# A gate's modulation moved ahead of the FFN, weight buffers that start their turn anew, and a second set of banks

## The chip, the cores and the metric

The kernel runs on one core of one Trainium2 chip. The time is that of the device, in microseconds (us), for one execution on that core. The engines are named as the profile names them: PE (TensorE, matmuls), DVE (VectorE), ACT (ScalarE), POOL (GpSimd) and SP (SyncE, which here only issues transfers). PEld is the loading of PE's weights.

## The reference

One block of an encoder: 512 tokens, width 2048. A vector `c` gives six modulation vectors. The block mixes tokens by two kinds of attention (global with grouped keys, and over a neighbourhood in a grid), merges both with sigmoid gates, projects the result with `w_out`, and adds a gated feed-forward net (FFN) of width 5632.

```python
c_act = jax.nn.silu(c)
mod = c_act @ w_ada[l] + b_ada[l]
sh1, sc1, g1, sh2, sc2, g2 = [m[:, None, :] for m in jnp.split(mod, 6, axis=-1)]
h = rms_norm(x, norm1_w[l]) * (1.0 + sc1) + sh1
...
merged = jax.nn.sigmoid(ga) * (ya @ w_oa[l]) + jax.nn.sigmoid(gb) * (yb @ w_ob[l])
x = x + g1 * (merged @ w_out[l])
h2 = rms_norm(x, norm2_w[l]) * (1.0 + sc2) + sh2
ff = (jax.nn.silu(h2 @ w_ffn_gate[l]) * (h2 @ w_ffn_up[l])) @ w_ffn_down[l]
x = x + g2 * ff
return rms_norm(x, final_w)
```

`g2`, the second gate, is 2048 numbers: `c_act` (2048) times a 2048 x 2048 part of `w_ada`, which is 16 MB. It is needed only at the very end, when the FFN's result is added.

## The kernel before

**Arithmetic.** Each fp32 product is made of three matmuls on split numbers (`mm3`, L140 to L143): hi times hi, hi times lo, lo times hi. A weight unit of 512 KB is loaded into a buffer `raw` by a DMA on SP's queue (L148); ACT copies it to the high half of a buffer `whl` (L133), DVE subtracts that for the low half (L134), and 24 matmuls of 128x512 use it.

**Buffers and their turn.** `buffer` (L106 to L111) counts the tiles taken of a tag. There are four `raw` and three `whl` buffers in the pool `wp`. From w_out on, a second pool `wq` (L730) adds one `raw` and two `whl`, so that the turn runs over five of each; the counter goes on from where it stands, and the last numbers of a turn are those in `wq`. The memory of `wq` was that of `p_y`: the attention outputs `y0` to `y15` and the scratch tiles `o` of the heads' projections.

**Order of the work.** The program is one list of instructions, which a scheduler turns into one queue for each engine; every engine works its queue in order. Work that isn't part of the main flow is put in generators (`bg`), and `pump` (L166) advances them by `pace["steps"]` at each weight unit or call; `soon` holds closing steps, to be run a given number of pumps later.

**Stages by time (from the profiled execution).** Input projections and the first modulation to about 260 us; global attention to 560; neighbourhood attention and gates to about 905. Then the heads' output projections (L715 to L727): 16 calls, each of 48 matmuls (two weight units), whose results DVE multiplies with the gates (L710), adds (L721) and splits into `m0` to `m7` (L726 and L727 for the last). Then w_out (L805 to L814): four passes over column blocks of 512, `cc` 0 to 3, where the units of a pass take one of `m0` to `m7` each. After it come the norm and the FFN's hidden layer in an arrangement that saves matmuls (seven products instead of eight, whose input sums `ta` and `tb` are formed from weights on DVE), from about 1310 to 2150. The first down pass (L1118 to L1125) is four column passes of four units each, each filling four banks of PSUM that ACT copies out (L1120). The groups of the down projection follow, to 2480, and the last part with the norm to the end.

**The second gate.** `ada_gate` (L320) makes one quarter (512 columns) of a gate: an accumulator `acc` is cleared by POOL, its first row set to the bias by a DMA, eight loads of 512 KB each (L274) bring two blocks of 128 rows, and DVE adds each, times `c_act`, into `acc` (L298). At the end one matmul with ones sums over the partitions (`total`). The first gate runs so beside the attention, loaded on SP's queue. The second ran during the FFN: loads on POOL's queue, one load ahead of its use, one accumulator, totals in bank T, and one advance at each step of a group's inner loop but the first two.

Of the kernel before, what the change touches and what calls it, by code (L numbers as in the profile page):

```python
# [13 lines left out]
F32 = mybir.dt.float32  # L14
F32R = mybir.dt.float32r
AF = mybir.ActivationFunctionType
# [3 lines left out]
P = 128  # L20
D = 2048
T = 512
NT = T // P
KT = D // P
# [63 lines left out]
def encoder_block(ctx: ExitStack, tc, xp, xT, c, w_ada, ada1_w, b_ada, norm1_w, w_in, q_norm_w, k_norm_w, tb,  # L88
                  w_oa, w_ob, w_out, norm2_w, w_gate, w_up, w_down, final_w, rope, wmask, out):
    nc = tc.nc  # L90
    V, S, G = nc.vector, nc.scalar, nc.gpsimd
# [30 lines left out]
    def bank(tag):  # L122
        return ps.tile([P, 512], F32, tag=tag, name=tag, bufs={"mm": 4, "S": 2, "T": 1, "Y": 1}[tag])
# [34 lines left out]
    bg = []  # L158
# [4 lines left out]

    pace = {"steps": 1}

    def pump():  # L166
        due = [f for n, f in soon if n <= 0]
        soon[:] = [(n - 1, f) for n, f in soon if n > 0]
        for f in due:
            f()  # L170
        if later:
            later.pop(0)()
        for _ in range(pace["steps"]):
            advance()
# [84 lines left out]
    t2 = const.tile([P, KT], F32, name="t2")  # L259

    accp = aside
    ada_room = {"bank": "Y", "bufs": 2, "ahead": 0, "queue": nc.sync}

    def ada_units(cols, w):

        nj = len(cols)
        nk = 1024 // (nj * w)

        def load(k0):
            raw = raw_tile()  # L270
            r4 = raw.rearrange("p (k c n) -> p k c n", k=nk, c=nj)
            for j, col in enumerate(cols):
                src = w_ada[k0 * P:(k0 + nk) * P, col:col + w]
                ada_room["queue"].dma_start(r4[:, :, j], src.rearrange("(k p) n -> p k n", p=P))  # L274
            return [(k0 + e, raw[:, e * nj * w:(e + 1) * nj * w]) for e in range(nk)]

        ready = []
        for k0 in range(0, KT, nk):
            ready.append(load(k0))
            yield ready.pop(0) if len(ready) > ada_room["ahead"] else None  # L280
        yield from ready

    def ada_acc(cols, w, bias):


        acc = accp.tile([P, 512], F32, tag="acc", name="acc", bufs=ada_room["bufs"])[:, :len(cols) * w]
        if bias:
            G.memset(acc, 0.0)
            nc.sync.dma_start(acc[0:1, :], b_ada[:, cols[0]:cols[0] + w])
        for parts in ada_units(cols, w):  # L290
            if parts is None:
                yield None
                continue
            for k, part in parts:
                if k == 0 and not bias:
                    V.tensor_scalar(acc, part, cact[:, k:k + 1], None, op0=ALU.mult)
                else:
                    V.scalar_tensor_tensor(acc, part, cact[:, k:k + 1], acc, op0=ALU.mult, op1=ALU.add)  # L298
            yield None
        yield acc  # L300
# [21 lines left out]
    def ada_gate(col, q, dst):  # L322

        for acc in ada_acc((col + q * 512,), 512, True):
            if acc is None:
                yield

        def total():
            y = bank(ada_room["bank"])
            nc.tensor.matmul(y, ones, acc, start=True, stop=True)  # L330
            o = io.tile([P, 512], F32, tag="io", name="ada_o")
            V.tensor_copy(o[0:1, :], y[0:1, :])
            nc.sync.dma_start(dst[q], o[0:1, :])

        soon.append((ada_room["bufs"] - 1, total))
        if ada_room["bufs"] == 1:
            yield

    def rows(dst, src):
        for q in range(4):  # L340
# [260 lines left out]
    bg.extend(ada_mod(3 * D, 4 * D, k, 2, (s2, b_sc2, n2, t2, b_sh2)) for k in range(0, KT, 2))  # L601
    g1_d, g2_d = ([dram.tile([1, 512], F32, name=f"g{n}d{q}") for q in range(4)] for n in (1, 2))
    bg.extend(ada_gate(2 * D, q, g1_d) for q in range(4))
    pace["steps"] = 2
    gates(sg_b, GB, 0, 8)
    pace["steps"] = 1
# [105 lines left out]
        return evac  # L712

    turn = itertools.cycle(("mm", "mm", "S"))
    for j in range(0, KT, 2):  # L715
        ma, mb = [], []
        for w, ys, sg, to in ((w_oa, yT[:8], sg_a, ma), (w_ob, yT[8:], sg_b, mb)):
            tag = next(turn)
            form1([w], j * P, 2, ys, [[bank(tag), bank(tag)]], gated(sg[j:], to))
        for e in range(2):  # L720
            V.tensor_add(ma[e], ma[e], mb[e])  # L721
            (mh, ml), o3 = (t.t for t in mT[j + e]), ma[e].rearrange("p (t n) -> p t n", t=2)
            if j + 2 < KT:
                split(mh, ml, o3)
            else:
                V.tensor_copy(mh, o3)  # L726
                V.tensor_sub(ml, o3, mh)  # L727
    p_y.release()
    aside.release()
    wq = tc.alloc_tile_pool(name="wq", bufs=1, side="right", reuse_waits="tile")  # L730

    x2_d = dram.tile([P, NT, D], F32, name="x2d")
# [83 lines left out]
        pump()  # L816
    norm((2, 3))
    gpool.release()
    accp = tc.alloc_tile_pool(name="accp", bufs=1, side="left", reuse_waits="tile")
    ada_room.update(bank="T", bufs=1, ahead=1, queue=nc.gpsimd)  # L820

# [62 lines left out]
    def group7(wsrc, xs, order, dst):  # L886

        bk = {r: bank(BANK[r]) for r in ORDER}
        for n, s in enumerate(order):
            w = wsrc(s)  # L890
            if n > 1:
                pump()
            for r in ORDER:
                (wh, wl), (xh, xl) = w[r], xs[s][r]
                for q in range(2):
                    for c in range(2):
                        o = bk[r][:, c * 256:(c + 1) * 256]
                        cs = slice(c * P, (c + 1) * P)
                        first, last = n == 0 and q == 0 and c == 0, n == len(order) - 1 and q == 1
                        mm3(o, wh[:, q, cs], wl[:, q, cs], xh[:, q], xl[:, q], first, last, skip_group_check=True)  # L900
        p = {r: b.rearrange("p (c n) -> p c n", c=2) for r, b in bk.items()}
        (d11, d12), (d21, d22) = dst
        with tc.high_priority():
            p1 = io.tile([P, 512], F32, tag="io", name="p1").rearrange("p (c n) -> p c n", c=2)
            S.activation(p1, p[1], AF.Copy)
            V.tensor_add(d11, p[2], p1)
            V.tensor_add(d21, p[6], p1)
            V.tensor_add(d12, p[5], d21)
            V.tensor_add(d12, p[3], d12)  # L909
            V.tensor_add(d21, p[7], d21)  # L910
            V.tensor_add(d22, p[5], d21)
            V.tensor_sub(d21, d21, p[4])
# [60 lines left out]
        e1, _ = c_tile(F32R, "e1")  # L973
        early[1] = ff_pair(0, 1, [e1[:, :1024], e1[:, 1024:]], nc.sync)

    bg.extend(ada_gate(5 * D, q, g2_d) for q in range(4))
    for n in range(FU):
        cs = []
        for w in (w_gate, w_up):
# [19 lines left out]
            V.tensor_mul(cs[1][:, sl], cs[1][:, sl], cs[0][:, sl])  # L999
        (nc.sync if n < FU - 1 else nc.gpsimd).dma_start(ff_d[n], cs[1])  # L1000

    while bg or soon:
        pump()
    wbufs["at"] = 0
    for p in (c_p, f_x[1], f_x[0], ca, f_x[3], f_x[2], accp, p_m):
        p.release()
    p_s = form_pool("p_s", "left")
    p_e = form_pool("p_e", "right")
# [108 lines left out]
    xs = FF(0, early, 48)  # L1117
    for cc in range(4):  # L1118
        o = acc_tile()
        form2(w_down, cc * 512, xs, lambda i, b: S.activation(o[:, i], b, AF.Copy), r0=0)  # L1120
        nc.gpsimd.dma_start(acc_d[cc], o)
        if cc == 0:
            xs.pairs.pop(0)
            xs.pairs.pop(1)
            bg.extend(sforms(j, 2 + j) for j in range(3))  # L1125
# [134 lines left out]
```

## Time and profile before

| what | value |
|---|---|
| time, median of 3 runs | 2630.73 us (2626.41 to 2637.36) |
| time of the profiled execution | 2638.57 us |
| its span in the profile | 2636.8 us |
| mean granted clock of PE | 0.993 |
| DVE, ACT, POOL busy | 73%, 39%, 5% of the span |
| transfers | 458.78 MB, mean 174 GB/s |

The profile's page gives busy times by engine, the chain of work that ended last, and groups of instructions. Windows give the same busy times for stretches of time, with the clock that PE was granted there (1.00 is full speed). Waits name what an engine stood still for. In the timeline a bracket shows how long the engine was idle before a row and what ended it.

### The profile page before, as it was taken

How to read it: one execution, taken by the hardware profiler on the slowest of the kernel's cores; microseconds unless marked ns; L12 is line 12 of the kernel's file. 1: busy time of each engine (PE TensorE's matmuls, PEld its weight loads, DVE VectorE, ACT ScalarE, POOL GpSimd, SP SyncE). 2: the span in 40 equal slices, each digit the busy share in tenths (PEclk: the TensorE clock that was granted, in tenths of full speed). 3: DMA queues.
4: the chain of work that ended last, by engine and by line, in shares of the span. 5: the costliest groups of instructions: out<-in, count | busy, mean ns of one | idle time of the engine just before them, and what ended most of it. 6: DMA issues, size and time to landing. Idle time of an engine off the chain costs nothing.

```text
span 2636.8 us, 40994 instructions
## 1 busy us (share of the span) xinstructions
PE 2575.5 (98%) x16569; PEld 2328.0 (88%) x16569; DVE 1912.8 (73%) x2710; ACT 1030.0 (39%) x1404; POOL 119.0 (5%) x166
## 2 busy tenths in 40 slices
PE   6999999999999999999999999999999999999998
PEld 5788888888788888788999999999999988999997
DVE  7985786666746544336798888888888875678767
ACT  5223544223333332226744444444444453434233
POOL 0100000001010000011000000000000000000000
PEclk9999999999999999999999999999999999999999
DMA  8864245974735844546454444444444456447473
GB/s 323 305 236 144 65 156 175 294 232 148 229 104 169 262 156 144 180 131 218 123 161 144 129 144 152 131 142 136 137 146 150 145 167 216 160 156 236 153 255 104
DMA packets 247855, 458.78 MB, mean 174 GB/s; under 512 B 16113, under 2 KB 102497, under 8 KB 239217
## 3 DMA queue, kind: packets, MB, share of 16 engines
q1 hardware_dynamic: 229504, 364.86, 43.1%
q0 software_dynamic: 16672, 88.09, 9.8%
q10 hardware_dynamic: 1488, 3.20, 0.3%
q8 instruction: 130, 2.13, 0.3%
q14 instruction: 61, 0.49, 0.1%
HBM read 412.03 MB, written 44.06 MB: 173 GB/s over the span
## 4 chain that ended last, share of the span: by engine, by line
PE 86%; DVE 6%; DMA 5%; issue 1%; ACT 1%; SPq 0%; DVEq 0%; ACTq 0%; POOLq 0%
PE mm L141 18%; PE mm L142 18%; PE mm L143 18%; PE S L141 6%; PE S L143 6%; PE S L142 6%; PE Y L141 3%; PE Y L142 3%; PE Y L143 3%; DVE whl L134 2%; DMA raw<-in_w_in 2%; DMA raw<-in_w_up 1%; DVE acc L298 1%; PE T L143 1%; PE T L142 1%
## 5 line engine op out<-in xcount | busy, mean ns | idle before, releaser
L133 ACT ACTIVATE whl<-raw 128x1024 fp32r<-128x1024 f32 (+1 forms) x483 | 464.5, 963 | 893.3 <-PE mm L143 302.9
L134 DVE TENSOR_TENSOR whl<-raw,whl 128x1024 fp32r<-128x1024 f32 (+1 forms) x483 | 532.7, 1114 | 312.1 <-ACT whl L133 302.2
L298 DVE SCALAR_TENSOR_TENSOR acc<-raw,cact,acc 128x512 f32<-128x512 f32 x248 | 187.2, 755 | 27.8 <-DMA raw<-in_w_ada 22.4
L133 ACT ACTIVATE whl<-tb 128x1024 fp32r<-128x1024 f32 x104 | 110.6, 1063 | 177.8 <-PE S L143 136.0
L133 ACT ACTIVATE whl<-ta 128x1024 fp32r<-128x1024 f32 x104 | 110.5, 1062 | 163.6 <-PE mm L143 123.0
L134 DVE TENSOR_TENSOR whl<-ta,whl 128x1024 fp32r<-128x1024 f32 x104 | 127.4, 1225 | 39.8 <-ACT whl L133 39.8
L134 DVE TENSOR_TENSOR whl<-tb,whl 128x1024 fp32r<-128x1024 f32 x104 | 127.0, 1221 | 15.3 <-ACT whl L133 14.7
L851 DVE TENSOR_TENSOR ta<-raw 128x512 f32<-128x512 f32 x104 | 71.9, 691 | 65.5 <-DMA raw<-in_w_down 36.9
L852 DVE TENSOR_TENSOR ta<-raw,ta 128x512 f32<-128x512 f32 x104 | 71.7, 690 | 42.9 <-DMA raw<-in_w_down 22.2
L141 PE MATMUL mm<-whl,a 128*128 128x256 f32 (+1 forms) x304 | 98.5, 325 | 3.7 <-ACT acc L1120 3.7
L142 PE MATMUL mm<-whl,a 128*128 128x256 f32 (+1 forms) x304 | 98.5, 324 | 1.5 <-DVE whl L134 1.5
L143 PE MATMUL mm<-whl,a 128*128 128x256 f32 (+1 forms) x304 | 98.2, 323 | 0.0
L141 PE MATMUL mm<-x3h,whl 128*128 128x256 f32 x336 | 94.3, 281 | 1.9 <-DVE c L909 1.9
L141 PE MATMUL mm<-x56h,whl 128*128 128x256 f32 x336 | 94.3, 281 | 0.5
L142 PE MATMUL mm<-x3l,whl 128*128 128x256 f32 x336 | 94.1, 280 | 0.0
L143 PE MATMUL mm<-x3h,whl 128*128 128x256 f32 x336 | 94.1, 280 | 0.0
L142 PE MATMUL mm<-x56l,whl 128*128 128x256 f32 x336 | 94.0, 280 | 0.0
L143 PE MATMUL mm<-x56h,whl 128*128 128x256 f32 x336 | 94.0, 280 | 0.0
L141 PE MATMUL S<-x56h,whl 128*128 128x256 f32 x336 | 94.0, 280 | 0.0
L142 PE MATMUL S<-x56l,whl 128*128 128x256 f32 x336 | 94.0, 280 | 0.0
L143 PE MATMUL S<-x56h,whl 128*128 128x256 f32 x336 | 94.0, 280 | 0.0
L142 PE MATMUL mm<-whl,s 128*128 128x256 f32 x320 | 90.4, 282 | 2.5 <-DVE whl L134 2.5
(1480 smaller groups left out, 8531.5 us busy)
## 6 DMA issues: line engine op xcount, KB each, us to landing
raw<-in_w_in SPq DMA_DIRECT2D x133, 512.0 KB
raw<-in_w_gate SPq DMA_DIRECT2D x92, 512.0 KB
raw<-in_w_up SPq DMA_DIRECT2D x88, 512.0 KB
raw<-in_w_down SPq DMA_DIRECT2D x88, 512.0 KB
raw<-in_w_ada SPq DMA_DIRECT2D x128, 256.0 KB
raw<-in_ada_w POOLq DMA_DIRECT2D x29, 1024.0 KB, 5.6
raw<-in_w_out SPq DMA_DIRECT2D x48, 512.0 KB
raw<-in_w_ada SPq DMA_DIRECT2D x32, 512.0 KB
```

What stands on the lines that cost most here:

```text
L133: S.activation(hi, src, AF.Copy)
L134: eng.tensor_sub(lo, src, hi)
L141: nc.tensor.matmul(o, lh, rh, start=start, stop=False, **kw)
L142: nc.tensor.matmul(o, lh, rl, start=False, stop=False, **kw)
L143: nc.tensor.matmul(o, ll, rh, start=False, stop=stop, **kw)
L298: V.scalar_tensor_tensor(acc, part, cact[:, k:k + 1], acc, op0=ALU.mult, op1=ALU.add)
L851: V.tensor_sub(t1, b12, b11)
L852: V.tensor_sub(t2_, b22, t1)
```

## The change

It has three parts.

1. The second gate's four generators are put into `bg` right after the first gate's, so they run when those are done. A list `paces` sets the number of advances of the next pumps: 0 and 1 in turn for the 32 pumps of the heads' projections, which makes 16 advances there, one a call; the other 16 come with the units of w_out's first two passes, one a unit. Loads are on SP's queue, with two accumulators in `gpool` and totals in bank Y. The special settings of the FFN (`ada_room`, the load ahead, the pool `accp`, the pump in the inner loop) are gone.
2. When `wq` is opened, the counters of `raw` and `whl` are set to -1, so the first unit of w_out takes number 0: the first four `raw` and the first three `whl` of w_out are in `wp`.
3. In the first down pass the banks alternate by column pass: four of tag mm in passes 0 and 2, two S, T and Y in passes 1 and 3.

```diff
@@ pump
+    paces = []
+
     def pump():
+        if paces:
+            pace["steps"] = paces.pop(0)
@@ the modulation
     accp = aside
-    ada_room = {"bank": "Y", "bufs": 2, "ahead": 0, "queue": nc.sync}
...
-                ada_room["queue"].dma_start(r4[:, :, j], src.rearrange("(k p) n -> p k n", p=P))
-            return [(k0 + e, raw[:, e * nj * w:(e + 1) * nj * w]) for e in range(nk)]
-
-        ready = []
-        for k0 in range(0, KT, nk):
-            ready.append(load(k0))
-            yield ready.pop(0) if len(ready) > ada_room["ahead"] else None
-        yield from ready
+                nc.sync.dma_start(r4[:, :, j], src.rearrange("(k p) n -> p k n", p=P))
+            yield [(k0 + e, raw[:, e * nj * w:(e + 1) * nj * w]) for e in range(nk)]
...
-        soon.append((ada_room["bufs"] - 1, total))
-        if ada_room["bufs"] == 1:
-            yield
+        soon.append((1, total))
@@ before the gates of the neighbourhood heads
     bg.extend(ada_gate(2 * D, q, g1_d) for q in range(4))
+    bg.extend(ada_gate(5 * D, q, g2_d) for q in range(4))
@@ heads' output projections
     turn = itertools.cycle(("mm", "mm", "S"))
+    paces.extend([0, 1] * KT)
...
     aside.release()
+    taken.update({t: -1 - taken[t] for t in ("raw", "whl")})
     wq = tc.alloc_tile_pool(name="wq", bufs=1, side="right", reuse_waits="tile")
@@ after w_out
     gpool.release()
-    accp = tc.alloc_tile_pool(name="accp", bufs=1, side="left", reuse_waits="tile")
-    ada_room.update(bank="T", bufs=1, ahead=1, queue=nc.gpsimd)
@@ FFN
             w = wsrc(s)
-            if n > 1:
-                pump()
...
-    bg.extend(ada_gate(5 * D, q, g2_d) for q in range(4))
...
-    while bg or soon:
-        pump()
@@ first down pass
-        form2(w_down, cc * 512, xs, lambda i, b: S.activation(o[:, i], b, AF.Copy), r0=0)
+        form2(w_down, cc * 512, xs, lambda i, b: S.activation(o[:, i], b, AF.Copy), r0=0,
+              tags=("S", "S", "T", "Y") if cc % 2 else ("mm",) * NT)
```

**Where the rows stand.** ACT at the entry of w_out, before. The numbers are the program's counters of tiles. `whl_8914` is the last unit of the heads; w_out's units 0, 1 and 2 are `whl_8979`, `whl_9008` and `whl_9037`, units 3 and 4 `whl_9071` and `whl_9100`:

```order
L133 ACTIVATE whl_8914<-raw_8912 128x1024
L133 ACTIVATE whl_9008<-raw_9006 128x1024
L133 ACTIVATE whl_9037<-raw_9035 128x1024
L133 ACTIVATE whl_8979<-raw_8977 128x1024
L133 ACTIVATE whl_9071<-raw_9069 128x1024
L133 ACTIVATE whl_9100<-raw_9098 128x1024
```

The same place after. `whl_8985` is the last unit of the heads; units 0 to 5 of w_out are `whl_9054`, `whl_9090`, `whl_9123`, `whl_9166`, `whl_9199` and `whl_9232`:

```order
L133 ACTIVATE whl_8985<-raw_8983 128x1024
L133 ACTIVATE whl_9054<-raw_9052 128x1024
L133 ACTIVATE whl_9090<-raw_9088 128x1024
L133 ACTIVATE whl_9166<-raw_9164 128x1024
L133 ACTIVATE whl_9199<-raw_9197 128x1024
L133 ACTIVATE whl_9123<-raw_9121 128x1024
L133 ACTIVATE whl_9232<-raw_9230 128x1024
```

Before, unit 0 came behind units 1 and 2; now units 0 and 1 are first, and unit 2 is behind units 3 and 4.

SP at the same place, before; `raw_8912` is the last load of the heads, `raw_8977` belongs to unit 0 of w_out, and `g` are the gates' tiles:

```order
L148 DMA raw_8912<-in_w_ob 128x4x256
L706 DMA g_8803<-sgb13_261 128x512
L706 DMA g_8873<-sga14_246 128x512
L148 DMA raw_9006<-in_w_out 128x2x512
L148 DMA raw_9035<-in_w_out 128x2x512
L706 DMA g_8877<-sga15_247 128x512
L706 DMA g_8941<-sgb14_262 128x512
L148 DMA raw_9069<-in_w_out 128x2x512
L148 DMA raw_9098<-in_w_out 128x2x512
L706 DMA g_8945<-sgb15_263 128x512
L148 DMA raw_8977<-in_w_out 128x2x512
```

And after, from unit 1 (`raw_9088`) to unit 2 (`raw_9121`); loads of `in_w_ada` are the second gate's:

```order
L148 DMA raw_9088<-in_w_out 128x2x512
L276 DMA raw_9117<-in_w_ada 128x2x512
L276 DMA raw_9160<-in_w_ada 128x2x512
L148 DMA raw_9164<-in_w_out 128x2x512
L698 DMA g_9020<-sgb15_263 128x512
L276 DMA raw_9193<-in_w_ada 128x2x512
L148 DMA raw_9197<-in_w_out 128x2x512
L148 DMA raw_9230<-in_w_out 128x2x512
L276 DMA raw_9259<-in_w_ada 128x2x512
L148 DMA raw_9121<-in_w_out 128x2x512
```

Unit 0's load (`raw_9052`) moved from the end of this stretch to four rows ahead of it; the gate's loads stand between the units, and unit 2's load is now the one at the end.

PE at the step from column pass 0 to 1 of the first down pass, before:

```order
L141 MATMUL mm_20362<-whl_20456,a1_20350 128x512
L142 MATMUL mm_20362<-whl_20456,a1_20350 128x512
L143 MATMUL mm_20362<-whl_20456,a1_20350 128x512
L141 MATMUL mm_20493<-whl_20499,a0_20351 128x512
L142 MATMUL mm_20493<-whl_20499,a0_20351 128x512
```

And after:

```order
L141 MATMUL mm_20358<-whl_20452,a1_20346 128x512
L142 MATMUL mm_20358<-whl_20452,a1_20346 128x512
L143 MATMUL mm_20358<-whl_20452,a1_20346 128x512
L141 MATMUL S_20489<-whl_20495,a0_20347 128x512
L142 MATMUL S_20489<-whl_20495,a0_20347 128x512
```

The first bank of pass 1 was of tag mm, of which pass 0 uses all four; now it is of tag S.

More of the change, by code (lines that the diff above doesn't have):

```diff
@@ L267, in ada_units @@
         nk = 1024 // (nj * w)
-        def load(k0):
+        for k0 in range(0, KT, nk):
             raw = raw_tile()
@@ L273, in load @@
                 src = w_ada[k0 * P:(k0 + nk) * P, col:col + w]
-                ada_room["queue"].dma_start(r4[:, :, j], src.rearrange("(k p) n -> p k n", p=P))
-            return [(k0 + e, raw[:, e * nj * w:(e + 1) * nj * w]) for e in range(nk)]
-        ready = []
-        for k0 in range(0, KT, nk):
-            ready.append(load(k0))
-            yield ready.pop(0) if len(ready) > ada_room["ahead"] else None
-        yield from ready
+                nc.sync.dma_start(r4[:, :, j], src.rearrange("(k p) n -> p k n", p=P))
+            yield [(k0 + e, raw[:, e * nj * w:(e + 1) * nj * w]) for e in range(nk)]
     def ada_acc(cols, w, bias):
-        acc = accp.tile([P, 512], F32, tag="acc", name="acc", bufs=ada_room["bufs"])[:, :len(cols) * w]
+        acc = accp.tile([P, 512], F32, tag="acc", name="acc", bufs=2)[:, :len(cols) * w]
         if bias:
@@ L290, in ada_acc @@
         for parts in ada_units(cols, w):
-            if parts is None:
-                yield None
-                continue
             for k, part in parts:
@@ L328, in total @@
         def total():
-            y = bank(ada_room["bank"])
+            y = bank("Y")
             nc.tensor.matmul(y, ones, acc, start=True, stop=True)
@@ L1000, in encoder_block @@
         (nc.sync if n < FU - 1 else nc.gpsimd).dma_start(ff_d[n], cs[1])
-    while bg or soon:
-        pump()
     wbufs["at"] = 0
-    for p in (c_p, f_x[1], f_x[0], ca, f_x[3], f_x[2], accp, p_m):
+    for p in (c_p, f_x[1], f_x[0], ca, f_x[3], f_x[2], p_m):
         p.release()
```

## The prediction

> **What bounds the kernel now.** I read the page first, its busy times and its chain of waits, then a table of windows by stage, then the waits of PE, then the timeline at the two longest waits.
>
> ```profile
> span 2636.8 us, 40994 instructions
> PE 2575.5 (98%) x16569; PEld 2328.0 (88%) x16569; DVE 1912.8 (73%) x2710; ACT 1030.0 (39%) x1404; POOL 119.0 (5%) x166
> PE 86%; DVE 6%; DMA 5%; issue 1%; ACT 1%; SPq 0%; DVEq 0%; ACTq 0%; POOLq 0%
> ```
>
> PE is busy 98% of the span and carries 86% of the chain. The change takes no matmul away (the four totals of the gate, a few matmuls in all, move but stay), so all that it can win is time in which PE waits or runs slowly. The windows, with their columns, say where that is:
>
> ```profile
> core 0: us, PE busy (x) PEld busy (x) DVE busy (x) ACT busy (x) POOL busy (x), PEclk, DMA share, GB/s
> 260.00:560.00 300.00, 297.20 (x1479) 243.11 (x1478) 225.77 (x433) 118.05 (x220) 4.25 (x3) 1.00 0.57 182
> 905.00:1080.00 175.00, 175.00 (x772) 144.55 (x771) 74.65 (x90) 47.63 (x56) 0.00 (x0) 1.00 0.47 147
> 1080.00:1310.00 230.00, 223.83 (x1170) 191.65 (x1170) 123.81 (x156) 110.83 (x163) 21.27 (x15) 0.99 0.53 169
> 1310.00:2150.00 840.00, 835.54 (x7119) 831.98 (x7118) 724.51 (x918) 362.45 (x384) 26.89 (x39) 1.00 0.46 143
> 2150.00:2250.00 100.00, 96.33 (x441) 80.33 (x440) 58.04 (x64) 42.07 (x51) 7.61 (x15) 0.97 0.62 211
> ...
> 1085.23:1092.06 6.83, 5.21 (x11) 3.64 (x12) 5.02 (x5) 3.23 (x4) 0.00 (x0) 0.50 0.62 178
> 2174.08:2180.91 6.83, 6.04 (x14) 4.79 (x15) 5.00 (x8) 4.35 (x8) 1.08 (x2) 0.50 0.77 240
> 1050.00:1100.00 50.00, 43.83 (x182) 35.26 (x181) 20.61 (x26) 10.45 (x11) 0.00 (x0) 0.93 0.55 176
> 1100.00:1150.00 50.00, 50.00 (x222) 41.40 (x222) 14.66 (x13) 12.47 (x18) 5.13 (x4) 1.00 0.50 163
> ```
>
> The heads' projections (905 to 1080) have no idle PE at all; w_out (from 1080) loses about 6 us, the FFN (1310 to 2150) 4.5 us of 840, the first down pass (2150 to 2250) 3.7 us. Behind the two long waits the granted clock is 0.50 for 6.83 us. Where 128x512 matmuls run undisturbed, 50 us hold 222 starts, so one takes 50 / 222 = 0.225 us and a unit of 24 takes 5.41 us.
>
> ```profile
> PE mm L141 <- ACT whl L133: 5.9, 1, 5.9
> PE mm L142 <- DVE whl L134: 5.1, 4, 2.5
> PE mm L141 <- ACT acc L1120: 3.7, 1, 3.7
> PE mm L141 <- ACT c L984: 2.1, 1, 2.1
> PE mm L141 <- DVE c L909: 1.9, 3, 1.0
> ```
>
> These are five of PE's waits (total, times, longest). The first is the entry of w_out, the third the step from column pass 0 to 1 of the first down pass, the last two lie in the FFN. The change reaches those four.
>
> **Weight buffers' turn at w_out.** The timeline at the end of the heads' projections:
>
> ```profile
> 1077.99 0.37 SPq L148 DMA_DIRECT2D raw<-in_w_out  x1
> ...
> 1080.29 0.39 PE L143 MATMUL mm<-y15h,whl 128*128 128x512 f32 x1
> 1080.71 1.06 ACT L133 ACTIVATE whl<-raw 128x1024 fp32r<-128x1024 f32 x1 [15.21 <-PE mm L143]
> ...
> 1083.19 1.29 DVE L727 TENSOR_TENSOR m7l<-o,m7h 128x512 fp32r<-128x512 f32 x2
> 1084.39 5.89 DVE L134 TENSOR_TENSOR whl<-raw,whl 128x1024 fp32r<-128x1024 f32 x5
> 1084.56 3.90 ACT L133 ACTIVATE whl<-raw 128x1024 fp32r<-128x1024 f32 x4 [2.79 <-DVE m7l L727]
> ...
> 1086.62 1.22 PE L141 MATMUL mm<-whl,m0h 128*128 128x512 f32 x2 [5.95 <-ACT whl L133]
> ```
>
> Before, the turn gives unit 0 (raw_8977) the new pool's raw buffer, over the y tiles, so it is loaded only at 1077.99; units 1 and 2 have their split weights over y and o, so ACT begins unit 1 only after the last head matmul (1080.71) and unit 2 only after m7l has been written (1084.56); unit 0's split stands behind both on ACT. PE starts 5.95 us late and then runs at half clock. By starts, 1050 to 1100 holds 182 where 222 fit: 40 x 0.225 = 9.0 us lost. The whole of it belongs to this entry, since the heads before it have no gap.
>
> What a load of 512 KB takes from issue to landing I read from the DMA issues in the FFN:
>
> ```profile
> raw<-in_w_ada POOLq DMA_DIRECT2D x32, 512.0 KB, 4.1
> ```
>
> After, units 0 and 1 have both buffers in the old pool. Unit 0's split buffer comes free two units before the end of the heads (about 1069.8), unit 1's one unit before (1075.3); I replay DVE's new order with the ada work in it (the last ada accumulations before each, two of 0.75 us a load) and get unit 0 split by about 1074 and unit 1 by about 1080, against needs at 1080.7 and 1086.1. What is late next is unit 2, whose raw buffer is now the one over the y tiles. On SP it stands behind unit 5 and an ada load that waits for a slot, so its DMA goes at about 1081; with 4.1 us to land it is there at 1085. On ACT it stands behind unit 4, which waits for m7l (1084.5, as before); hi is then done at 1084.56 + 2 x 1.06 = 1086.7. On DVE it stands behind the lo of units 3 and 4 at 5.89 / 5 = 1.18 us each: unit 2 complete at about 1088. PE needs it at 1080.7 + 2 x 5.41 = 1091.5, a margin of 3.5 us. So the likeliest is that the whole gap goes: **-9.0 us**; bounds 0 (the wait only changes units) and -9.0.
>
> **Two sets of banks in the first down pass.**
>
> ```profile
> 2170.81 0.39 PE L143 MATMUL mm<-whl,a 128*128 128x512 f32 x1
> 2174.87 0.80 PE L141 MATMUL mm<-whl,a 128*128 128x512 f32 x1 [3.67 <-ACT acc L1120]
> ```
>
> ```profile
> 2169.38 0.53 POOL L1042 DMA_DIRECT2D ffe<-ffd  x1 [7.12 <-DVE whl L134]
> ```
>
> ```profile
> 2169.52 0.62 ACT L133 ACTIVATE s<-ffe 128x512 fp32r<-128x512 f32 x1
> 2173.27 1.06 ACT L133 ACTIVATE s<-ffe 128x1024 fp32r<-128x1024 f32 x1 [3.13 <-DMA ffe<-ffd]
> 2174.24 1.07 ACT L1120 ACTIVATE acc<-mm 128x512 f32<-128x512 f32 x2
> ```
>
> Column pass 1 needs the four mm banks that pass 0 has just filled. Their copies stand on ACT behind `s<-ffe`, whose DMA was issued at 2169.38 and ends its wait at 2173.27, so PE stands 3.67 us and then has 6.83 us at 0.50. From 2174.87 to 2180.91 are 6.04 us with 14 starts, worth 14 x 0.225 = 3.15 us: 2.9 us more. Together 6.6 us. After, pass 1 writes S, S, T, Y, which the FFN's last group left free long before, and ACT's blocked queue no longer matters at that step. What is late next: the fourth weight unit of pass 1, whose split stays behind the copies on ACT. It would have to be done 3 units = 16.2 us after 2171.2, at 2187.4; ACT has six instructions of about 1 us between 2174.2 and it, so about 2181. Pass 2 takes mm again, 21.6 us after pass 0 ended. The following groups begin with mm while pass 3 sits in S, S, T, Y, and come to S only 48 short matmuls later. **-6.6 us**; bounds -3.7 (if the clock falls for another reason) and -6.6.
>
> **The second gate's modulation, moved.** 32 loads of 512 KB, 64 accumulations and four totals leave the FFN and go, on SP instead of POOL, one to each of 16 calls of the heads' projections and one to each of 16 units of w_out.
>
> ```profile
> L298 DVE SCALAR_TENSOR_TENSOR acc<-raw,cact,acc 128x512 f32<-128x512 f32 x64 | 48.0, 751 | 6.3 <-DMA raw<-in_w_ada 4.5 <-DMA acc<-in_b_ada 1.5
> ```
>
> In the FFN this takes 48.0 of DVE's 724.51 us away and 16 MB of the transfers. PE waits there for DVE's evacuations (c L909) 1.9 us in three places; with DVE's share down from 86% to 81% and the ada waits gone from its queue I take all of it: **-1.9 us** (bounds 0 and -1.9). The wait of 2.1 us (c L984) is at the FFN's start, where ACT's evacuation stands behind a split that waited for its load:
>
> ```profile
> 1314.28 1.06 ACT L133 ACTIVATE whl<-raw 128x1024 fp32r<-128x1024 f32 x1 [2.58 <-DMA raw<-in_w_up]
> ```
>
> That is no modulation load; ACT's rows there come in a slightly other order: 0, bounds -2.1 and +2.1.
>
> In the heads DVE goes from 74.65 to 74.65 + 32 x 0.75 = 98.7 us of 175 (56%), the transfers from 147 to 147 + 16 x 0.524 MB / 175 us = 195 GB/s. In w_out's first 87 us (16 units of 5.41) the same 24 us are added to a DVE that is busy 14.66 of 50, and 96 GB/s to 163. What covers both is the slack of the load ring; the row of 260 to 560 has the same pairing of weight and modulation loads at 182 GB/s and PE busy 297.20 of 300. I take 0, bounds 0 and +4. PE's four totals are the same matmuls in another place: 0. SP gains 32 issues, POOL loses them; POOL's new memsets of the accumulators wait for the totals, with nothing behind them before w_out's residuals. The scheduler also reorders some matmuls between 560 and 905 as a by-product: 0, bounds -1.5 and +1.5 as an estimate from 300 - 297.20 = 2.8 us of idle PE in the stage before.
>
> **The sum**: -9.0 - 6.6 - 1.9 = -17.5 us of the profiled run's 2638.57. That run lies 7.8 us above the median of 2630.73, still inside the runs shown (2626.41 to 2637.36). I put the same loss against the median: 2630.73 - 17.5 = 2613.2, so 2613 us, 0.7% faster. No measurement of this kernel tells much less than 0.5% (13.2 us) from no change, so the forecast is not far over that line.
>
> **What a short wait costs.** Rival A depends on it:
>
> ```profile
> 82.13 2.07 PE L435 MATMUL mm<-whl,h4h 128*128 128x512 f32 x4 [2.62 <-DVE whl L134]
> ```
>
> ```profile
> 81.70:85.10 3.40, 2.97 (x7) 2.39 (x8) 3.40 (x6) 0.73 (x1) 0.17 (x1) 0.50 0.67 229
> ...
> 1317.80:1321.20 3.40, 3.37 (x27) 3.28 (x28) 3.37 (x5) 3.40 (x6) 0.75 (x1) 1.00 0.52 163
> ```
>
> A wait of 2.62 us is followed by 3.40 us at clock 0.50, which costs 1.7 us more; the wait of 2.1 us before 1317.8 is followed by a full clock. So I charge a wait of about 2.5 us with 1.7 on top, and one of 4 to 6 us with 2.9. [...]
>
> **Rivals.**
> A: the gap at w_out moves to unit 2. Its raw load is behind two others on SP and shares the DMA engines with them, its split behind unit 4's. If the load takes over 4.1 + 3.5 = 7.6 us, PE waits. For: before, ACT's wait was for this very memory. Against: the margin of 3.5 us. A late 2.5 us costs 2.5 + 1.7 = 4.2: 2617.4; a full new gap gives the 9.0 back: 2622.2. I put its middle at 2619.
> B: the 9 us won at w_out come back at the FFN's start, where the wait behind c L984 hangs on a weight load; if those loads are bound by the transfers (0.53 of the engines busy over 1080 to 1310, and now with 8 MB more) and not by buffers that PE frees, PE arrives earlier at the same load: 2622. Against: 0.53 is far from full.
> C, slower: in w_out weight and ada loads take the same ring of five raw buffers in turn on one queue, and DVE's accumulation of an ada load stands ahead of the next unit's lo. If one load had to land before the next was issued, a unit would need 4.1 + 1.5 (two accumulations) + 1.06 + 1.18 = 7.8 us instead of 5.41: 16 x 2.4 = 38 us lost, 2613 + 38 = 2651. It decides from 17.5 / 16 = 1.1 us a unit. Against: five buffers let loads overlap, and 260 to 560 ran that way without it.
>
> **How the numbers follow.** My forecast 0.58, A 0.17, B 0.11, C 0.14. A is mostly within 0.5% (2617.6 to 2643.9), with its short form just faster; B is within; C is slower but for weak forms of it. That makes faster 0.60, same 0.28, slower 0.12. The range: below, 2613 less the two unknown terms (2.1 and 1.5) and about 5 for the scatter of a median of runs as far apart as those shown, 2604; above, through B (2622) and the weak end of C to the old median, 2632, beyond which most of C is left out. The forecast's own range is 2604 to 2618.
>
> **What would show it.** PE's wait `mm <- ACT whl` at the entry of w_out is gone and 1050 to 1100 holds about 222 starts at clock 1.00; a wait for whl two units later would be A. No `mm <- ACT acc` wait near 2155, and no half clock behind it. No L909 waits in the FFN, DVE there near 676 us. In 905 to 1080 PE stays fully busy at about 195 GB/s; waits for whl in w_out's first two passes with DMA raw<-in_w_ada ahead of DVE would be C. The forecast is wrong if a new PE wait over 2.5 us shows up anywhere between 905 and 1310, or if the w_out gain is missing at 1310.

## The result, and the profile after

The changed kernel takes 2599.29 us (median of 15 runs, 2592.71 to 2636.14), the kernel before 2633.23 us (15 runs, 2625.66 to 2642.89). The ratio is 0.9871, 95% interval [0.9855, 0.9887]: 1.3% faster, 34 us. The forecast was 2613 us, in the range of 2604 to 2632: the sign was right, the gain about twice what was forecast, and 2599 lies below the range. Of the 15 runs 13 lie between 2592.7 and 2607.4 and two at 2632.4 and 2636.1; those two are left out of the ratio and come up again below.

The stages, from the start of one stage's first matmul to the next, in the two traces (us):

| stage | before | after | difference |
|---|---|---|---|
| up to the heads' projections | 905.5 | 907.4 | +1.9 |
| heads' projections, with the wait at w_out's entry | 181.1 | 175.9 | -5.2 |
| w_out | 180.9 | 180.6 | -0.3 |
| first products of the FFN | 53.4 | 52.1 | -1.3 |
| FFN, from the first `x3h` matmul | 828.4 | 802.3 | -26.1 |
| first down pass | 93.9 | 87.1 | -6.8 |
| rest | 393.7 | 392.0 | -1.7 |
| span | 2636.8 | 2597.5 | -39.3 |

The two gaps went about as forecast (the first stands in the table together with work that moved to it, see below). The FFN, from which the prediction expected 1.9 us, gave 26.1. The windows of the changed kernel, with the columns as before:

```profile
905.00:1080.00 175.00, 175.00 (x770) 144.15 (x769) 101.40 (x131) 49.84 (x61) 0.53 (x1) 1.00 0.63 206
1310.00:2118.00 808.00, 804.08 (x7073) 803.28 (x7072) 682.80 (x844) 358.81 (x380) 1.63 (x3) 1.00 0.42 128
1050.00:1100.00 50.00, 50.00 (x221) 41.26 (x221) 33.25 (x43) 12.81 (x13) 0.00 (x0) 1.00 0.71 237
1100.00:1150.00 50.00, 50.00 (x218) 40.74 (x217) 31.96 (x39) 12.22 (x17) 7.93 (x5) 1.00 0.89 311
2120.00:2210.00 90.00, 90.00 (x417) 75.22 (x416) 55.73 (x62) 39.97 (x50) 7.47 (x14) 1.00 0.66 227
```

PE has no idle time in the heads, at w_out's entry (221 starts in 50 us, clock 1.00) or in the first down pass. PE's waits from 1310 to 2118 are all at the FFN's start, and c L909's are gone:

```profile
PE mm L143 <- DVE whl L134: 1.8, 1, 1.8
PE mm L141 <- ACT whl L133: 1.1, 2, 0.9
PE mm L141 <- ACT c L973: 1.0, 1, 1.0
```

In these two traces idle PE time in the FFN is about the same: 840 - 835.54 = 4.5 us before, 808 - 804.08 = 3.9 after. So hardly any of the 26 us are waits. They are in the starts: in 50 us without a wait, of which none shows idle PE, the kernel before makes 427 matmuls and later 443; the changed kernel makes 443 or 444 everywhere. Before, three windows:

```profile
1450.00:1500.00 50.00, 50.00 (x427) 50.00 (x426) 41.44 (x53) 21.31 (x22) 0.73 (x1) 1.00 0.44 132
1850.00:1900.00 50.00, 50.00 (x427) 50.00 (x426) 40.63 (x52) 21.92 (x23) 0.00 (x0) 1.00 0.44 138
2050.00:2100.00 50.00, 50.00 (x443) 50.00 (x443) 43.54 (x55) 20.72 (x22) 0.00 (x0) 1.00 0.47 149
```

After, the same three:

```profile
1450.00:1500.00 50.00, 50.00 (x444) 50.00 (x443) 40.43 (x50) 22.09 (x24) 0.00 (x0) 1.00 0.37 110
1850.00:1900.00 50.00, 50.00 (x443) 50.00 (x442) 43.12 (x55) 22.09 (x24) 0.00 (x0) 1.00 0.34 105
2050.00:2100.00 50.00, 50.00 (x444) 50.00 (x443) 41.63 (x51) 24.04 (x26) 0.00 (x0) 1.00 0.47 147
```

In the start times of these two traces a matmul of 128x256 takes 117.8 ns from start to start at the one pace and 113.3 ns at the other, with PE busy and the granted clock 1.00 at both. Sorted by the distance to the next start, the FFN before has 5371 matmuls at the slow pace and 1642 at the fast one, the changed kernel 3 and 7016: 5371 x 4.45 ns = 23.9 us, nearly the whole difference. The slow pace before begins at 1319.8 and ends at 1936.0, at the third total of the gate; it returns for a dozen matmuls after each of two waits, and to stay at the fourth total, at 2129.

The rest is made of smaller terms. The four totals, each of which held the stream up by 0.86 us, left the FFN with the gate (3.4 us less, which come again in the heads and w_out). Waits of 1.9 us on c L909 went, and 2.0 us of waits stand at the start of the changed FFN. Behind the longest of these PE has 3.4 us at half clock, worth 1.7 us, which the window of 808 us rounds away:

```profile
1319.14 0.38 PE L143 MATMUL mm<-m5h,whl 128*128 128x256 f32 x1 [1.81 <-DVE whl L134]
```

```profile
1319.68:1323.10 3.42, 3.42 (x18) 3.42 (x17) 3.42 (x6) 0.00 (x0) 0.00 (x0) 0.50 0.50 153
```

Together 23.9 + 3.4 + 1.9 - 2.0 - 1.7 = 25.5 us of the 26.1.

### The profile page after: what moved, and what is told of

It is laid out like the page before. It is cut to its first block, busy times and chain, and to the rows that moved or that the text cites. A ratio compares the mean times of both kernels' runs of the same rounds, so it can differ in the third digit from the quotient of the medians.

```text
span 2597.5 us, 40993 instructions
## 1 busy us (share of the span) xinstructions
PE 2545.6 (98%) x16569; PEld 2300.5 (89%) x16569; DVE 1917.5 (74%) x2710; ACT 1027.9 (40%) x1404; POOL 96.8 (4%) x134
## 4 chain that ended last, share of the span: by engine, by line
PE 76%; DMA 2%; DVE 2%; issue 2%; ACT 0%; POOL 0%; SPq 0%; DVEq 0%; POOLq 0%; ACTq 0%
PE mm L143 17%; PE mm L142 17%; PE mm L141 17%; PE S L141 5%; PE S L143 5%; PE S L142 5%; PE Y L141 2%; PE Y L142 2%; PE Y L143 2%; DMA raw<-in_w_down 1%; DVE whl L134 1%; DMA raw<-in_w_in 0%; PE T L143 0%; PE T L141 0%; PE T L142 0%
## 5 line engine op out<-in xcount | busy, mean ns | idle before, releaser
L142 PE MATMUL mm<-whl,s 128*128 128x256 f32 x320 | 89.6, 280 | 2.0 <-DVE whl L134 2.0
L141 PE MATMUL mm<-whl,s 128*128 128x256 f32 x320 | 89.5, 280 | 0.3 <-DVE acc L1102 0.3
L143 PE MATMUL mm<-whl,s 128*128 128x256 f32 x320 | 89.5, 280 | 0.0
L142 PE MATMUL mm<-whl,a 128*128 128x256 f32 (+1 forms) x240 | 72.1, 301 | 1.1 <-DVE whl L134 1.1
```

The source lines that it names most:

```text
L141: nc.tensor.matmul(o, lh, rh, start=start, stop=False, **kw)
L142: nc.tensor.matmul(o, lh, rl, start=False, stop=False, **kw)
L143: nc.tensor.matmul(o, ll, rh, start=False, stop=stop, **kw)
```

## The experiments

Two theories of the pace were set against each other. **Pace theory**: PE's stream of matmuls keeps the pace it has, 117.8 or 113.3 ns, until something disturbs it (a wait, a total), and each disturbance decides the pace anew. **Load theory**: the modulation's transfers and accumulations beside the FFN slow every matmul down. All ratios are against the kernel before, run on the same chip.

| run | median us (lowest to highest) | ratio, 95% interval | FFN in its trace, us | slow / fast matmuls there |
|---|---|---|---|---|
| turn_only | 2624.87 (2613.39 to 2628.92) | 0.9960 [0.9946, 0.9975] | 827.6 | 4481 / 2515 |
| banks_only | 2624.21 (2618.45 to 2635.14) | 0.9972 [0.9952, 0.9992] | 821.8 | 3405 / 3606 |
| gate_only | 2608.43 (2605.84 to 2632.74) | 0.9917 [0.9887, 0.9948] | 834.2 | 7011 / 0 |
| after_loads | 2619.29 (2612.48 to 2632.58) | 0.9948 [0.9928, 0.9969] | 815.0 | 2001 / 4993 |
| after_totals | 2622.01 (2613.79 to 2627.15) | 0.9959 [0.9944, 0.9974] | 822.8 | 3665 / 3352 |
| turn_banks | 2622.08 (2607.06 to 2627.93) | 0.9955 [0.9935, 0.9975] | 830.1 | 5978 / 1033 |
| gate_banks | 2601.16 (2596.76 to 2602.37) | 0.9883 [0.9864, 0.9902] | 800.3 | 3 / 7034 |
| before_swap | 2632.94 (2626.86 to 2642.80) | 1.0007 [0.9991, 1.0023] | 828.4 | 4487 / 2505 |
| steer1 | 2602.39 (2600.27 to 2603.74) | 0.9882 [0.9859, 0.9905] | 800.5 | 2 / 7035 |
| steer2 | 2599.83 (2596.25 to 2602.51) | 0.9870 [0.9849, 0.9891] | 802.1 | 5 / 7020 |

### The turn alone

```diff
--- before
     aside.release()
+    taken.update({t: -1 - taken[t] for t in ("raw", "whl")})
```

> The kernel before, with the buffers' turn restarted at w_out and nothing else. Two theories of the 26 us that the FFN (from the first x3h matmul to the first matmul of the down pass) became shorter. Pace theory: a dense stream of 128x256 matmuls on PE runs at one of two paces, 117.8 or 113.3 ns a matmul, and changes between them only where the stream is disturbed (a wait, a total). Load theory: the modulation's transfers and accumulations beside the FFN slow each matmul by 4.4 ns. Both: the 5.95 us wait at the entry of w_out and the half clock behind it go, 9 us less there; some of it may come back at the FFN's start. Load theory: the FFN keeps its 828 us, so about 2624 us. Pace theory: the disturbances at the FFN's start and at the four totals are met in another phase, the FFN is anywhere from 800 to 832 us, and its matmuls show both paces with switches at a total or a wait.

Heads and w_out together take 175.0 + 177.9 = 352.9 us instead of 362.0: 9.1 us less. The entry shows no wait and no half clock:

```profile
1050.00:1100.00 50.00, 50.00 (x223) 41.40 (x222) 22.80 (x27) 12.79 (x13) 0.00 (x0) 1.00 0.63 207
```

The FFN has both paces, changing at totals (1527, 1728, 1919) and at two waits on DVE's evacuation at about 1630, as the pace theory has it. In sum it is hardly shorter, which agrees with the load theory's time, so this run alone doesn't decide.

### The bank sets alone

```diff
--- before
-        form2(w_down, cc * 512, xs, lambda i, b: S.activation(o[:, i], b, AF.Copy), r0=0)
+        form2(w_down, cc * 512, xs, lambda i, b: S.activation(o[:, i], b, AF.Copy), r0=0,
+              tags=("S", "S", "T", "Y") if cc % 2 else ("mm",) * NT)
```

> The kernel before, with two bank sets in the first down pass and nothing else. Both theories: the wait of 3.67 us on ACT acc and the 6.8 us at half clock go, 6.6 us less, and the FFN ahead of it is untouched: 2626 to 2627 us. A wait of more than 1 us in column passes 1 or 2 would mean that the weight split behind the blocked copies became the next limit.

The first down pass takes 87.1 instead of 93.9 us, and PE waits for nothing in it:

```profile
2150.00:2200.00 50.00, 50.00 (x222) 41.42 (x221) 34.01 (x37) 25.27 (x30) 5.32 (x10) 1.00 0.75 252
```

The expectation that the FFN ahead of it would be untouched was missed: with the same program up to there, it took 821.8 us instead of 828.4 and had 3405 slow matmuls instead of 5371. The two executions met waits of different length, such as 2.6 us instead of 0.5 on c L909 at 1558, and left them at different paces.

### The gate alone

The whole diff but the lines of the two runs above.

> The kernel before, with the second gate's modulation moved among the heads' projections and w_out and nothing else. Load theory: the FFN's matmuls run at 113.3 ns throughout, 26 us less, and the two gaps at w_out's entry and in the down pass stay: about 2607 us. Pace theory: with no totals and hardly a wait in the FFN, one pace holds for the whole FFN, 113.3 ns (about 2607) or 117.8 ns (about 2633). By the prediction's own step (only the waits on c L909 go) it would be 2631.

Five runs took 2605.8 to 2610.2 us, the profiled one 2632.74. Its FFN ran slow from end to end, with no modulation load, accumulation or total beside it:

```profile
1450.00:1500.00 50.00, 50.00 (x427) 50.00 (x427) 39.53 (x51) 21.74 (x23) 0.00 (x0) 1.00 0.39 115
1850.00:1900.00 50.00, 50.00 (x427) 50.00 (x426) 38.78 (x49) 21.36 (x22) 0.00 (x0) 1.00 0.38 112
2050.00:2100.00 50.00, 50.00 (x427) 50.00 (x426) 40.86 (x50) 19.56 (x21) 0.00 (x0) 1.00 0.41 127
```

That rules out the load theory as the cause of the slow pace, and in this execution the gate's move won nothing. One program has two times, some 25 us apart, and 7011 x 4.45 ns = 31 us is what a whole FFN at the slow pace costs. That the five shorter runs had a fast FFN, and the changed kernel's two runs at 2632 and 2636 a slow one, is the likely reading; of none of them a trace was taken, so that is argued, not shown. Also unexpected: w_out's entry has hardly a wait here either (0.15 us), though the turn wasn't restarted.

### The gate's loads back in the FFN, without totals

```diff
--- after
+    def idle_gate(q):
+        acc = accp.tile([P, 512], F32, tag="acc", name="acc", bufs=1)
...
+                nc.gpsimd.dma_start(raw.rearrange("p (k n) -> p k n", k=2),
...
+                    V.scalar_tensor_tensor(acc, raw[:, e * 512:(e + 1) * 512], cact[:, k + e:k + e + 1], acc,
...
+    bg.extend(idle_gate(q) for q in range(4))
...
+            if n > 1:
+                pump()
```

> The changed kernel, with the second gate's 32 loads (POOL's queue, one ahead) and 64 accumulations put back into the FFN as extra work whose result is not used, without the four totals; the accumulator's 2 KB are taken where they were before. Load theory: the FFN's matmuls run at 117.8 ns again, the FFN is 26 us longer, about 2625 us. Pace theory: no total, so one pace from the FFN's start to its end but for waits; if it is 113.3 ns with all the loads beside it, the load theory is out; about 2600 us, or 2632 if the start is met in the other phase.

```profile
1450.00:1500.00 50.00, 50.00 (x444) 50.00 (x443) 42.59 (x55) 22.40 (x23) 1.25 (x2) 1.00 0.48 151
2050.00:2100.00 50.00, 50.00 (x427) 50.00 (x426) 42.47 (x54) 21.37 (x22) 0.00 (x0) 1.00 0.40 126
```

With all the loads beside it, PE makes 444 starts until 1895, at 151 GB/s in the first window. So the loads slowed no matmul there. They did bring short waits back: between 1700 and 1900 the stream is interrupted seven times, three of them by waits of 0.2 to 0.4 us for DVE's evacuations, and after the last PE was slow to the FFN's end. So in this trace the loads acted through the waits that came with them, which the expectation of one pace "but for waits" allowed; its times, 2600 or 2632, were missed by the median of 2619. In the trace (a run of 2613.97 us) the FFN is 12.7 us longer than in the changed kernel: 2001 slow matmuls are 8.9 us of it, and 1.7 us are half clock at its start, 6.83 us long instead of 3.41. That the other runs lost more in the same way is likely, but was not traced.

### Totals in the FFN, without loads

```diff
--- after
+    acc = accp.tile([P, 512], F32, tag="acc", name="acc", bufs=1)
+    G.memset(acc, 0.0)
...
+            if 2 * n + (w is w_up) in (5, 10, 15, 20):
+                V.tensor_copy(acc[:, :1], dst[1][1][:, 0, 0:1])
+                nc.tensor.matmul(bank("T"), ones, acc, start=True, stop=True)
```

> The changed kernel with four more totals in the FFN and no modulation loads there: a matmul of ones with a cleared accumulator (128x512 fp32, two passes), one in every fifth group, each after that group's evacuation, result not used. Each takes 0.63 us by the totals of before: 2.5 us. Pace theory: each total is a new draw, so stretches of 117.8 and 113.3 ns a matmul appear with their edges at the totals; the FFN comes out between 805 and 834 us and differs from run to run, a median of 2605 to 2625 us. If totals don't change the pace, the FFN keeps that of its start, 805 us in most runs, about 2602 us.

```profile
1450.00:1500.00 50.00, 50.00 (x427) 50.00 (x426) 38.28 (x47) 21.91 (x23) 0.00 (x0) 1.00 0.38 114
1550.00:1600.00 50.00, 50.00 (x444) 50.00 (x443) 43.08 (x56) 22.41 (x23) 0.00 (x0) 1.00 0.34 104
1850.00:1900.00 50.00, 50.00 (x444) 50.00 (x443) 41.32 (x53) 23.32 (x25) 0.00 (x0) 1.00 0.36 106
2050.00:2100.00 50.00, 50.00 (x427) 50.00 (x426) 42.91 (x54) 19.86 (x22) 0.00 (x0) 1.00 0.40 127
```

The pace turns from slow to fast at the total at 1518.5 and back at the one at 1901.5; at the other two it stays. Four totals, which hold the stream up by 1.0 to 1.3 us each in this trace (0.86 us each in the trace of before, not the 0.63 expected), move the median by 23 us against the changed kernel.

### Turn and banks, without the gate; gate and banks, without the turn

`turn_banks` is the kernel before with the diffs of turn_only and banks_only; `gate_banks` is the changed kernel without the line `taken.update(...)`.

> The changed kernel with the second gate left in the FFN (the turn and the bank sets changed). By the sum of the single parts: 9.1 and 6.8 us less than before and the FFN drawn anew at each total and wait, 2618 us, between 2605 and 2628. If this came out near 2599, moving the gate would be worth nothing.

> The changed kernel without the restart of the turn. With the gate moved alone no wait for weights showed at w_out's entry, though the restart was left out: the gate's own loads shift the turn. So the restart should be worth nothing on top of the gate: as the changed kernel, 2600 us within 3 us. If the restart is still needed, 9 us more: 2609.

Without the gate moved, the two gaps are gone and the time is 2622: the gate's move is worth the other 23 us. Without the restart it is 2601, within the changed kernel's interval. But the restart isn't idle: in the trace of gate_banks PE waits once at w_out's second unit, and from 1084 to 1100 the clock is 0.89 in the mean.

```profile
1094.24 0.79 PE L142 MATMUL mm<-whl,m1h 128*128 128x512 f32 x1 [3.16 <-DVE whl L134]
```

That is 5.0 us more in w_out than after (185.6 against 180.6): 3.2 of wait and 1.7 of half clock. gate_only, with the same order there, waits 0.15 us at that place. So without the restart the entry holds in some executions and not in others; how often was not counted. With it a smaller wait can come too, as steer1 shows below.

### Another order of the three matmuls

```diff
--- before
         nc.tensor.matmul(o, lh, rh, start=start, stop=False, **kw)
-        nc.tensor.matmul(o, lh, rl, start=False, stop=False, **kw)
-        nc.tensor.matmul(o, ll, rh, start=False, stop=stop, **kw)
+        nc.tensor.matmul(o, ll, rh, start=False, stop=False, **kw)
+        nc.tensor.matmul(o, lh, rl, start=False, stop=stop, **kw)
```

> The kernel before with the three matmuls of every split product in another order: hi hi, lo hi, hi lo instead of hi hi, hi lo, lo hi. The same weights are then never loaded twice in a row within a product. If the slow pace comes from that repeated load, no 128x256 stretch runs at 117.8 ns and the FFN takes about 805 us: 2610 us. If the slow pace has nothing to do with it, both paces appear as before: 2633 us within 8.

Ratio 1.0007 and both paces (4487 matmuls slow, 2505 fast): the slow pace doesn't come from loading the same weights twice in a row.

### Turning the pace on purpose

```diff
--- after
     def down_group(cc, ss, cl, acc, behind):
+        if cc == 0 and ss[0] == 2:
+            for _ in range(1):
+                tp = bank("mm")
+                for e in range(4):
+                    nc.tensor.transpose(tp[:, e * P:(e + 1) * P], ident, ident)
```

steer1 has `range(1)`, steer2 `range(2)`.

> The changed kernel with four transposes of the identity on PE (128x128, 0.11 us each, into a bank that is free, result not used) between the first down pass and the down groups. In all ten traces so far a 128x256 stream that follows a 128x512 stream without a wait starts at 117.8 ns, and at the FFN's entry sets of four transposes turn one pace into the other in a fixed pattern. Pace theory: the transposes may turn the first stretch of the down groups (some 1080 matmuls, to their first wait) to 113.3 ns, 4.8 us less for 0.4 us of transposes; if they don't, 0.4 us more. Any other theory (loads, contention) keeps 117.8 ns there.

> The same with eight transposes instead of four. In the FFN's entry the pattern needs one, two or three sets to reach the fast pace. Pace theory: at least one of four and eight transposes gives 113.3 ns in the first stretch of the down groups; 4.8 us less for 0.9 us. If both keep 117.8 ns, the pace is not set by what PE ran just before.

The same 60 us at the start of the down groups, in the changed kernel, in steer1 and in steer2:

```profile
2210.00:2270.00 60.00, 60.00 (x512) 60.00 (x511) 41.68 (x52) 22.60 (x24) 1.60 (x3) 1.00 0.49 161
```

```profile
2210.00:2270.00 60.00, 60.00 (x532) 60.00 (x531) 40.10 (x51) 23.09 (x25) 1.61 (x3) 1.00 0.50 166
```

```profile
2210.00:2270.00 60.00, 60.00 (x512) 60.00 (x511) 41.75 (x52) 22.19 (x24) 1.61 (x3) 1.00 0.45 151
```

Four transposes turn the pace there to 113.3 ns (532 starts), eight don't (512, as in the changed kernel). In steer1 nearly the whole rest stays fast: 36 slow matmuls after the boundary instead of 1109. And yet nothing is won: that stage takes 380.3 us to the last matmul, after 380.5. Between the column groups PE now waits for DVE's evacuation; this is steer1 from 2200 to 2510:

```profile
PE mm L141 <- DVE acc L1107: 4.7, 2, 3.1
PE S L141 <- ACT whl L133: 2.1, 1, 2.1
PE mm L142 <- DVE whl L134: 1.8, 3, 0.8
PE S L142 <- DVE whl L134: 1.7, 2, 1.1
```

These are 10.3 us, against 7.5 after in the same window, where the first of them (L1102 there) is 0.3. Behind the wait of 3.1 us the clock is 0.50 for 3.41 us, a stretch that the changed kernel does not have, worth 1.7 us. So 2.8 us of waits, 1.7 of half clock and 0.4 of transposes stand against the 4.8 us won. Neither steered kernel beats the changed one.

## Why the prediction was wrong

**The step that failed** is in the part on the second gate's modulation: "with DVE's share down from 86% to 81% and the ada waits gone from its queue I take all of it: -1.9 us (bounds 0 and -1.9)". The waits did go. But the sum counted only idle PE and half clock, and took a busy PE for a PE at its pace. The FFN's gain was 26.1 us in the two traces, nearly all of it from 5371 matmuls at 117.8 ns that now take 113.3. The bounds should have held the pace: up to the 23.9 us of the 5371 slow matmuls less if the whole FFN ran fast, and 1642 x 4.45 ns = 7.3 us more if it ran slow, as it did in gate_only's trace. The trace of before showed both paces, in windows of 50 us with 427 and with 443 starts and no idle PE in either. The prediction used starts per window for w_out and didn't read them for the FFN. In the trace of before the pace changed at interruptions of the stream alone: at the FFN's start, at its third and fourth total, and for a dozen matmuls behind each of two waits. In the changed kernel's trace, without totals, 7016 matmuls are fast and 3 slow. That its FFN comes out fast in most executions follows from nothing in the prediction and was not explained by the runs either, so the size of the gain is in part luck.

**The turn at w_out, -9.0 us.** Alone it gave 9.1. The rank of the late unit was right, its margin was not: unit 2 was to be complete at 1088 with 3.5 us to spare. In the changed kernel w_out begins at 1083.4; PE's first matmul of unit 2 is at 1094.24, and the second, at 1094.47, needs the low half. Unit 2's load was issued at 1084.80, ended ACT's wait at 1091.95, and its low half was done at 1094.27, in three views of the queues:

```profile
1084.80 0.46 SPq L148 DMA_DIRECT2D raw<-in_w_out  x1
```

```profile
1091.95 2.01 ACT L133 ACTIVATE whl<-raw 128x1024 fp32r<-128x1024 f32 x2 [2.17 <-DMA raw<-in_w_out]
```

```profile
1093.04 1.23 DVE L134 TENSOR_TENSOR whl<-raw,whl 128x1024 fp32r<-128x1024 f32 x1 [2.01 <-ACT whl L133]
```

The load took 7.15 us, not the 4.1 of the FFN's loads, beside other transfers (237 GB/s in that window), and was issued 1.4 us behind w_out's start instead of 0.3. Of the margin 0.2 us was left. That rival A did not come here is thus luck, and in steer1, whose program is the same up to there, it did come in a small form at unit 2:

```profile
1095.78 0.50 PE L141 MATMUL mm<-whl,m2h 128*128 128x512 f32 x1 [0.36 <-ACT whl L133]
1097.04 0.50 PE L142 MATMUL mm<-whl,m2h 128*128 128x512 f32 x1 [0.76 <-DVE whl L134]
```

Its price for a wait of some 3 us (the wait plus 1.7) was measured in gate_banks. And the 9.0 us are not the turn's alone: with the gate moved, most of the gap is gone without the restart too (gate_only).

**The bank sets, -6.6 us.** 6.8 in the trace of banks_only and of the changed kernel. That the fourth unit's split would still be in time held. That no measurement tells much less than 0.5% from no change was too careful: banks_only is 0.28% faster and its interval ends below 1.

**The moved work at 0.** Heads and w_out take 175.9 + 180.6 = 356.5 us after and 352.9 in turn_only, 3.6 us more. The four totals are 3.4 of them, at 0.86 us each, the same that the FFN lost; so in this trace the moved loads and accumulations cost next to nothing, as forecast. Together they hide part of the turn's gain in the table above. DVE in the heads has 101.40 us, forecast 98.7; the transfers 206 GB/s, forecast 195.

**The FFN's start and rival B.** The sum put the wait there (c L984, 2.1 us) at 0 with bounds of 2.1 either way. After, PE's waits at that place are 3.9 us, with 1.7 us of half clock behind them: 3.5 us more. B's reason, that PE arrives earlier at the same load, doesn't explain it, since turn_only, where PE arrives still earlier and the gate is not moved, waits 1.7 us there. All seven traces with the gate moved have 3.4 to 4.0 us; what in their order does it was not traced.

**Rival C** didn't come about: w_out shows no wait for ada loads. Rival C's condition, a load that must land before the next is issued, is not met: the load issued at 1084.80 ended ACT's wait at 1091.95, and the next load of `raw` was issued at 1089.79.

**The clock.** The prediction priced the half clock by the length of the wait: about 2.5 us brings it, 2.1 us does not. In gate_banks a wait of 3.16 us was followed by half clock, as the trace before showed for 2.62 us and 2.48 us. But in banks_only waits of 3.01 us and 2.64 us were followed by full clock, and in the changed kernel the half clock at 1319.68 came behind a wait of 1.81 us, with three shorter ones in the 8 us ahead of it. This is banks_only at the longer wait:

```profile
1319.06 0.38 PE L141 MATMUL mm<-m4h,whl 128*128 128x256 f32 x1 [3.01 <-ACT c L984]
```

```profile
1319.00:1326.00 7.00, 6.94 (x59) 6.84 (x60) 6.96 (x10) 5.78 (x9) 0.75 (x1) 1.00 0.52 150
```

So the length of one wait doesn't tell in these traces whether the clock falls.

## What to carry to other kernels

Busy time didn't say here how fast PE worked: it was 50.00 of 50 us with 427 matmuls and with 443. So count matmul starts per window, or the distance between them, in stretches without waits, and compare stretches of one kernel with each other before taking PE's busy share as a floor. A short interruption of a dense stream can cost far more than its own time if it leaves the stream at another pace: in after_totals four totals of 1.0 to 1.3 us each moved the median by 23 us against the changed kernel. So small helper matmuls are worth trying outside long dense stages. And a faster stretch can be worth nothing where the next wait sets the pace: in steer1 (380.3 us for the stage, after 380.5) it was paid back in waits for the evacuations and in the half clock behind one of them.

## What the runs showed of the hardware

A dense stream of 128x256 matmuls ran in these traces at one of two paces, 113.3 or 117.8 ns from start to start, with the granted clock at 1.00 and PE without idle time in both (before from 1450 to 1500: 427 matmuls in the window, after: 444); no third one was held at that clock. The pace didn't follow the transfers (fast at 151 GB/s in after_loads, slow at 112 in gate_only) or DVE's load beside it (42.59 us busy of 50 and 38.78 in the same two windows), nor the order of the three matmuls (both paces in before_swap, 4487 slow and 2505 fast). In the traces of before and after it changed only where the stream was interrupted.

After the 20 totals in the FFN in the traces of before, turn_only, banks_only, turn_banks and before_swap the pace was fast six times and slow 14 times. In all 20 the first of the total's two passes took 433 or 434 ns from start to start ahead of a fast stretch and 428 or 429 ns ahead of a slow one (before: 428, 429, 434 and 428, with a fast stretch behind the third alone); in after_totals, whose totals stand behind a copy on DVE, it took 529 to 534 ns without such an order. A 128x256 stream that followed a 128x512 stream without a wait began slow in all ten traces that have it undisturbed (after from 2210 to 2270: 512 matmuls in the window); four transposes in between made it fast (steer1: 532), eight did not (steer2: 512). At the FFN's entry, from 1282 on in before and from 1278 on in after, eight sets of four transposes, about 24 matmuls apart, left the pace fast, fast, slow, slow, fast, slow, slow and fast, the same in both traces.

What makes the two paces, and why that of the changed kernel's FFN comes out fast in most executions (13 of 15 by their times), was not settled.
